# Raw x transposed before the row factor, small loads on ScalarE's queue, and a new order for a planned kernel

## The chip, the cores and the metric

The kernel runs on 1 core of one Trainium2 chip. The metric is the time of one execution in microseconds on the device, lower is better. The time before is 354.06 us, the median of 3 runs.

## The reference

A trunk of two layers on x (256 tokens, width 1024): an RWKV-7 time mixing with 16 heads of 64, and a block-sparse attention that, with 256 tokens and blocks of 256, is plain causal attention within one block. All in float32. What matters here, cut:

```python
def rms_norm(x, g):
    y = xf * lax.rsqrt(jnp.mean(xf * xf, axis=-1, keepdims=True) + RMS_EPS)
    return y * g
...
def rwkv7_time_mix(h, mu, w_in, ...):            # h = rms_norm(x, norm_a)
    xx = jnp.pad(h, ((0, 0), (1, 0), (0, 0)))[:, :-1] - h        # the token before, minus this one
    # six inputs (h + xx * mu[i]) @ w_in[...]: r, w (64 wide), k, v, a (64 wide), gate
    w = -softplus(-(w0 + tanh(wdn) @ w2)) - 0.5;  decay = exp(-exp(w))
    a = sigmoid(a0 + adn @ a2)
    ...                                           # kk normed per head, k scaled by a
    def step(S, inp):                             # a scan over the 256 tokens, state 64 x 64 per head
        S = S * d_t - (S kk_t) b_t + v_t k_t;  y = S r_t
    ...                                           # group norm, bonus, silu gate
    return y @ w_out
...
x = x + rwkv7_time_mix(rms_norm(x, norm_a), ...)
kb, vb, kmean = shared_kv(x, ...)                 # rms_norm(x) @ w_kv
x = x + moba_attention(rms_norm(x, norm_b), ...)  # (softmax(q k) v * silu(gate)) @ w_out
```

## The kernel before

The work is written as some hundreds of small generators ("parts"). Each yields operations, events and buffer requests; a planner, the class Weave, runs them against a model of the engines while the kernel is built, and emits each operation when its model starts it. So the order of the instructions on every engine, and which of two engines takes an operation that may go to either, come from the planner's costs, from the priority with which a part is spawned (lower first) and from a table of numbers (PR) and a few constants (ORDER_A, FIRST, ALT, STICK, WARM and others) at the end of the file. On the chip the order is fixed: every engine runs its list from the front, and waits where an operand is not ready. One line (L308) issues nearly all VectorE, ScalarE and GpSimd instructions, L413 the products, L417 the transposes on TensorE, L424 the loads; so rows are told apart by the names of their tiles.

The tokens are two blocks of 128 (b = 0, 1), the columns two halves of 512 (n or q = 0, 1), called halves of the heads.

*The head.* block(b) squares x's two halves on ScalarE (sq, with the sum in ssq), adds the two sums on VectorE (rs) and takes the power -1/2 on GpSimd. In the kernel before, normed(b, q, r) multiplies x by that factor (xn), transposes xn on TensorE in four pieces, and multiplies by norm_a while it copies the result to hT (tokens along the free axis; VectorE for q = 0, ScalarE for q = 1). xxT is hT of the token before minus hT. start() turns the rows of norm_a and mu_a into columns (vrow to vT), and forms wm, the two 64-wide weights wl times mu. The low-rank products (low_rank) take hT with wl and xxT with wm, 16 per block, and the "rate" products w2x with their result give decay (sw) and a (ia).

*The mixed inputs.* For the key k, z = hT + xxT * mu is formed per block and 256 rows (u, SCALAR_TENSOR_TENSOR) and split into a high part (zhi, ScalarE, rounded to fp32r) and a low part (zlo, VectorE). The weights come in quarters of 256 x 512 (raw), split in the same way (whi, wlo). A dense job sums three products per tile: whi zlo, wlo zhi, whi zhi. The input v is not split but multiplied in plain fp32 ("raw" with zhi and zlo as places).

*The rest.* Each half of the heads goes through transposes of alpha (the tile called sw by then), the forms M1 and M2 (kkh and ia) and rho (eL), products within chunks of 64 tokens (WL, BK), the inverse of the triangular matrices (XF, tmp, xw on VectorE; ZX, QS on TensorE, with products of 16, 32 and 64 rows), and the recurrence over four chunks. Then come the output projection, the sums (x), K, V, Q and gate, the scores, softmax, values, and the last projection. warm_up() fills TensorE with products of zeros at the beginning. Loads go out on SyncE's queue in the planner's order, and a load into a buffer waits there until the buffer is free.

*Names:* whi/wlo, zhi/zlo: high and low parts; con: the constants (identity in its first 128 columns); acc and ps: PSUM buffers; rs: row factor; bv: a vector spread over all partitions.

## Time and profile before

| | before |
|---|---|
| median of 3 runs | 354.06 us (353.94 to 358.91) |
| profiled execution | 354.56 us |
| its span, first to last instruction | 352.7 us |
| TensorE busy (PE) | 342.2 us, 97% |
| VectorE busy (DVE) | 286.6 us, 81% |
| ScalarE busy (ACT) | 211.1 us, 60% |
| GpSimd busy (POOL) | 46.7 us, 13% |
| chain that ended last, by engine | PE 82%, DVE 13%, DMA 1%, issue 1% |

Busy times count an instruction from its start to its modelled end, and neighbours overlap; where a row gives 0.39 us for a product, the next one may start 0.23 us later. A row of a timeline gives the start, the length and, in brackets, the idle time of the engine before it and what ended it. [...] A plain fp32 product of the program appears as two records.

### The profile page before, as it was taken

Reading aid. Unit: us, or ns where it says so; the run is one execution under the profiler, and the core shown is the slowest. Engines: PE = TensorE matmul, PEld = TensorE weight load, DVE = VectorE, ACT = ScalarE, POOL = GpSimd, SP = SyncE. Lnnn points to the kernel's source line nnn. Section 1 sums busy time; section 2 is a strip of 40 time slices with the busy share of each in tenths; the row PEclk is TensorE's granted clock in tenths of the full one; section 3 lists DMA queues with packets and bytes.
Section 4 is the critical chain, followed back from the end, with each engine's and each line's share of the span. In section 5 each row is a group of like instructions: output and inputs, shape, how many; then the busy total and the mean of one; then the engine's idle time right before and its main releaser. Section 6 shows DMA issues by size and latency. Waiting matters only on the chain.

```text
span 352.7 us, 7611 instructions
## 1 busy us (share of the span) xinstructions
PE 342.2 (97%) x3006; PEld 266.1 (75%) x3006; DVE 286.6 (81%) x572; ACT 211.1 (60%) x415; POOL 46.7 (13%) x71
## 2 busy tenths in 40 slices
PE   8798999999999999999999999999999999999995
PEld 8774877778466775568777788788888878889784
DVE  2899789999999869959769989648868987769823
ACT  5379986754247852265673556645578775688620
POOL 1200050000310000200220522005504005000000
PEclk9899999999999999999999999999999999999999
DMA  7674762673254912356535512565540266503603
GB/s 197 179 205 137 240 192 77 171 215 94 89 151 125 239 59 61 91 134 233 189 111 180 187 60 73 198 222 185 175 164 2 77 228 223 190 1 122 205 35 119
DMA packets 29740, 51.44 MB, mean 146 GB/s; under 512 B 4412, under 2 KB 5764, under 8 KB 29704
## 3 DMA queue, kind: packets, MB, share of 16 engines
q1 hardware_dynamic: 29704, 50.94, 47.4%
q8 instruction: 24, 0.39, 0.5%
q14 instruction: 12, 0.10, 0.1%
HBM read 48.31 MB, written 1.05 MB: 140 GB/s over the span
## 4 chain that ended last, share of the span: by engine, by line
PE 82%; DVE 13%; DMA 1%; issue 1%; POOL 0%; ACT 0%; SPq 0%; DVEq 0%
PE acc L413 56%; PE ps L413 19%; PE ps L417 6%; DVE u L308 3%; DVE wlo L308 2%; DVE zlo L308 1%; DMA tri<-in_consts_dram 1%; DVE z L308 1%; DVE k L308 1%; DVE x L308 1%; DVE xxT L308 1%; DVE tmp L308 1%; DVE kkh L308 1%; DVE XF L308 0%; POOL rs L308 0%
## 5 line engine op out<-in xcount | busy, mean ns | idle before, releaser
L308 DVE TENSOR_TENSOR wlo<-raw,whi 128x1024 fp32r<-128x1024 f32 x70 | 85.4, 1222 | 25.2 <-ACT whi L308 25.0
L308 ACT ACTIVATE whi<-raw 128x1024 fp32r<-128x1024 f32 x70 | 74.1, 1064 | 39.4 <-PE acc L413 23.7
L413 PE MATMUL acc<-wlo,zhi 128*128 128x512 f32 x120 | 51.6, 430 | 1.0 <-DVE wlo L308 1.0
L413 PE MATMUL acc<-whi,zlo 128*128 128x512 f32 x120 | 47.1, 393 | 0.6 <-DVE zlo L308 0.6
L413 PE MATMUL acc<-whi,zhi 128*128 128x512 f32 x120 | 47.1, 392 | 0.0
L413 PE MATMUL acc<-whi,z 128*128 128x512 f32 x128 | 39.8, 392 | 0.0
L413 PEld LDWEIGHTS acc<-wlo,zhi 128*128 128x128 f32 x120 | 22.5, 188 | 7.3 <-DVE wlo L308 1.4
L413 PEld LDWEIGHTS acc<-whi,z 128*128 128x128 f32 x128 | 24.1, 188 | 4.9
L413 PEld LDWEIGHTS acc<-whi,zhi 128*128 128x128 f32 x120 | 22.5, 188 | 5.0
L413 PEld LDWEIGHTS acc<-whi,zlo 128*128 128x128 f32 x120 | 22.6, 189 | 4.8 <-DVE zlo L308 0.9
L413 PE MATMUL acc<-wlo,z 128*128 128x512 f32 x64 | 26.0, 406 | 0.0
L413 PE MATMUL acc<-zb,whi 128*128 128x256 f32 x128 | 23.3, 282 | 0.0
L413 PE MATMUL acc<-whi,zb 128*128 128x512 f32 x64 | 20.0, 394 | 0.0
L413 PE MATMUL acc<-whi,zf 128*128 128x512 f32 x64 | 19.8, 390 | 0.0
L413 PEld LDWEIGHTS acc<-zb,whi 128*128 128x128 f32 x128 | 19.7, 189 | 0.1
L413 PE MATMUL acc<-zb,wlo 128*128 128x256 f32 x64 | 18.9, 295 | 0.0
L308 POOL TENSOR_TENSOR nrm<-nrm,half 128x8 f32<-128x8 f32 x4 | 8.1, 2021 | 78.0 <-DVE nrm L308 78.0
L413 PE MATMUL acc<-raw,zlo 128*128 128x512 f32 x32 | 15.5, 605 | 0.0
L413 PE MATMUL acc<-raw,zhi 128*128 128x512 f32 x32 | 15.0, 606 | 0.0
L413 PEld LDWEIGHTS acc<-wlo,z 128*128 128x128 f32 x64 | 12.1, 189 | 2.9 <-issue 0.5
L413 PEld LDWEIGHTS acc<-whi,zb 128*128 128x128 f32 x64 | 12.1, 189 | 2.6
L308 ACT ACTIVATE zhi<-u 128x256 fp32r<-128x256 f32 (+1 forms) x16 | 7.9, 522 | 10.1 <-DVE u L308 7.0
(215 smaller groups left out, 721.6 us busy)
## 6 DMA issues: line engine op xcount, KB each, us to landing
raw<-in_w_in_a_dram SPq DMA_DIRECT2D x32, 512.0 KB, 4.3
raw<-in_w_kv_dram SPq DMA_DIRECT2D x16, 512.0 KB, 3.7
raw<-in_w_in_b_dram SPq DMA_DIRECT2D x16, 512.0 KB, 4.2
raw<-in_w_out_a_dram SPq DMA_DIRECT2D x8, 512.0 KB, 4.9
raw<-in_w_out_b_dram SPq DMA_DIRECT2D x8, 512.0 KB, 4.5
x<-in_x_dram SPq DMA_DIRECT2D x8, 256.0 KB, 4.4
out_dram<-x SPq DMA_DIRECT2D x8, 128.0 KB, 1.9
NBK<-kkh SPq DMA_DIRECT2D x6, 128.0 KB, 5.8
```

What stands on the lines that cost most here:

```text
L308: op = Op(eng, us, lambda: getattr(obj, name)(*a, **k), table=table, banks=banks(*a, *k.values()), port=port(eng, name, us, a, k))
L413: return us, lambda: nc.tensor.matmul(dst, l, r, **kw), size(r) * (1 if l.dtype == F32R else 4) * min(l.shape[0], size(l)) / P, banks(dst) ...
L417: return max(0.045, 0.1085 * src.shape[0] / P), lambda: nc.tensor.transpose(dst, src, idt), 256 * src.shape[0] / P, banks(dst), src.shape[ ...
```

## The change

The row factor is put on after the transpose. turned(b, q) transposes raw x as soon as it is there and multiplies by norm_a on the way to hT; block(b) turns the row factor itself into a row, spread over all partitions (pr, one transpose), and normed(b, q, rT) multiplies hT by it in place, on VectorE. The loads of norm_a, mu_a and the identity are issued on ScalarE's queue, ahead of its table load. More parts take their priority from the table; the table, the job order of the first layer's v and g, that of the second layer, and the planner's constants have other values; warm_up() takes an acc buffer instead of a ps buffer. The step from 16 to 32 rows of the inverse is not changed, only the planner's cost of some of its products (0.031 to 0.033).

```diff
+    for a, b in ((vrow[0:8], norm_a[0].rearrange("(a p) -> a p", p=P)),
+                 (vrow[8:56], mu_a[0].rearrange("i (a p) -> (i a) p", p=P)), (con[:, 0:128], consts[0:P, 0:128])):
+        nc.scalar.dma_start(a, b)
+    warm = keep((P, 1), "warm")
+    nc.scalar.activation(warm, half[:, 0:1], AF.Tanh)
...
-            spawn(fetch(f"x{n}{b}", (xb[n, b], x2[b * P:(b + 1) * P, hs(n)])), -3)
+            spawn(fetch(f"x{n}{b}", (xb[n, b], x2[b * P:(b + 1) * P, hs(n)])), PR["x"] if b else -3)
...
-            spawn(load(i, raw, op), (-2.5, PR["raw1"], PR["raw2"])[i] if i < 3 else 0)
+            spawn(load(i, raw, op), PR[f"raw{i}"] if i < 5 else 0)
...
-    def normed(b, q, r):
+    def turned(b, q):
+
+        b1 = slice(b * P + 1, (b + 1) * P + 1)
+        yield event("ident")
+        yield event(f"x{q}{b}")
+        pt = yield bank
+        yield tr4(pt, xb[q, b])
+        yield event("vT")
+        yield either(V.tensor_tensor(hT[q][:, :, b1], pt.rearrange("p (a t) -> p a t", t=P), bc(na_T[:, q * 4:q * 4 + 4], P), op=ALU.mult),
+                     several([S.activation(hT[q][:, i, b1], pt[:, i * P:(i + 1) * P], AF.Copy, scale=na_T[:, q * 4 + i:q * 4 + i + 1])
+                              for i in range(4)]))
+        bank.give(pt)
+        fire(f"turned{b}{q}")
+
+    def normed(b, q, rT):
...
-        xn = T_(f"k2{q}{b}", "xn")
-        yield either(V.tensor_scalar(xn, xb[q, b], r, None, op0=ALU.mult), S.activation(xn, xb[q, b], AF.Copy, scale=r))
...
+        yield event(f"turned{b}{q}")
+        yield V.tensor_tensor(hT[q][:, :, b1], hT[q][:, :, b1], rT[:, 0:P].unsqueeze(1).to_broadcast([P, 4, P]), op=ALU.mult)
...
     def block(b):
+        for q in range(2):
+            spawn(turned(b, q), PR["block"] * b + 1)
         r = yield from norm_row(b)
-        yield event("vT")
-        for q in range(2):
-            spawn(normed(b, q, r), 1 + b)
+        pr = yield accs
+        yield pe(tr(pr[:, 0:P], r.to_broadcast([P, P]), ident))
+        ends = [spawn(normed(b, q, pr), PR["block"] * b + 1 + q * 0.1) for q in range(2)]
+        for e in ends:
+            yield e
+        accs.give(pr)
...
-PR = {"raw1": 2.8, "raw2": 95.8, "w2x": 25.7, "first": -19.5, "k0": -26.6, "r0": -29.4, "k1": 147.2, "r1": -16.2,
+PR = {"x": 26.1, "wl": -2.1, "raw0": 26.7, "raw1": 29, "raw2": 76.5, "raw3": -21.5, "raw4": 31.2, "lora": 56.8,
...
-ORDER_A = ("k0", "r0", "k1", "r1", "v0", "g0", "v1", "g1")
-FIRST = [(0, 1), (0, 0), (1, 1), (2, 1), (1, 0), (2, 0), (3, 0), (3, 1)]
+ORDER_A = ("k0", "r0", "k1", "r1", "v0", "v1", "g0", "g1")
+FIRST = [(0, 1), (0, 0), (1, 1), (1, 0), (2, 1), (2, 0), (3, 1), (3, 0)]
...
-COLD, WINDOW, KEEP, WARM = 1.9, 3.4133, 1046, (1.1, 9.16)
+COLD, WINDOW, KEEP, WARM = 1.9, 3.4133, 874, (1.1, 11.52)
...
-SWAP, STICK = 0.1, 0
+SWAP, STICK = 0.1, 56.9
```

VectorE's list at the very beginning, before (x_74 and x_76 are block 0, x_75 and x_77 block 1; hT_83 is the first half of the columns, xxT_85 its difference):

```order
L308 TENSOR_TENSOR rs_141<-ssq_98 128x1
L308 COPY vT_81<-ps_50_149 128x56
L308 TENSOR_SCALAR xn_153<-x_74,rs_141 128x512
L308 TENSOR_SCALAR xn_154<-x_76,rs_141 128x512
L308 TENSOR_TENSOR hT_83<-ps_54_160,vT_81 128x4x128
L308 TENSOR_TENSOR xxT_85<-hT_83 128x4x128
L308 TENSOR_TENSOR rs_177<-ssq_99 128x1
L308 SCALAR_TENSOR_TENSOR u_58_185<-xxT_85,vT_81,hT_83 128x128
L308 TENSOR_TENSOR xxT_86<-hT_84 128x4x128
L308 SCALAR_TENSOR_TENSOR u_58_185<-xxT_85,vT_81,hT_83 128x128
L308 SCALAR_TENSOR_TENSOR u_59_186<-xxT_85,vT_81,hT_83 128x128
L308 TENSOR_SCALAR xn_198<-x_75,rs_177 128x512
```

and now (x_72 and x_74 are block 0, x_73 and x_75 block 1; hT_86 and hT_87 the two halves, acc_53 the turned factor of block 0, rs_232 the factor of block 1):

```order
L308 COPY vT_84<-ps_49_138 128x56
L308 TENSOR_TENSOR rs_148<-ssq_101 128x1
L308 TENSOR_TENSOR hT_86<-ps_48_137,vT_84 128x4x128
L308 TENSOR_TENSOR hT_87<-ps_51_140,vT_84 128x4x128
L308 TENSOR_TENSOR hT_86<-hT_86,acc_53_158 128x4x128
L308 TENSOR_TENSOR hT_87<-hT_87,acc_53_158 128x4x128
L308 TENSOR_TENSOR xxT_88<-hT_86 128x4x128
L308 TENSOR_TENSOR wm_176<-wl_78,vT_84 128x8x64 x2
...
L308 TENSOR_TENSOR zlo_116<-u_62_202,zhi_115 128x2x128
L308 COPY vT_84<-ps_60_196 128x16
L308 TENSOR_TENSOR rs_232<-ssq_102 128x1
L308 TENSOR_TENSOR hT_86<-ps_67_234,vT_84 128x4x128
```

The steps on xn are gone, both halves of hT are formed on VectorE and multiplied there a second time, and the factor of block 1 stands behind the splits (zlo) of block 0, not in the middle of its work.

SyncE's list of loads, before (con_73 the identity, vrow_78 the rows of norm_a and mu_a, x_75 and x_77 block 1, raw_34, raw_35 and raw_36 the first three weight quarters):

```order
L424 DMA x_74<-in_x_dram 128x512
L424 DMA x_76<-in_x_dram 128x512
L424 DMA con_73<-in_consts_dram 128x128
L424 DMA vrow_78<-in_norm_a_dram 8x128
L424 DMA vrow_78<-in_mu_a_dram 48x128
L424 DMA x_75<-in_x_dram 128x512
L424 DMA x_77<-in_x_dram 128x512
L424 DMA wl_80<-in_w_in_a_dram 128x8x64 x2
L424 DMA raw_34_105<-in_w_in_a_dram 128x2x512
L424 DMA bv_33_104<-in_ka_a_dram 128x512
L424 DMA vrow_79<-in_norm_kv_dram 8x128
```

and now (x_73 and x_75 block 1, raw_34 and raw_35 the first two quarters; the third, raw_36, stands at place 25, behind raw_74 and raw_78, the fourth and fifth):

```order
L424 DMA x_72<-in_x_dram 128x512
L424 DMA x_74<-in_x_dram 128x512
L424 DMA wl_78<-in_w_in_a_dram 128x8x64 x2
L424 DMA bv_33_107<-in_ka_a_dram 128x512
L424 DMA vrow_77<-in_norm_kv_dram 8x128
L424 DMA vrow_77<-in_norm_b_dram 8x128
L424 DMA x_73<-in_x_dram 128x512
L424 DMA x_75<-in_x_dram 128x512
L424 DMA bv_59_188<-in_kk_a_dram 128x512
L424 DMA raw_34_108<-in_w_in_a_dram 128x2x512
```

Three small loads have left the list; wl, a bv and the two later gains stand ahead of block 1 of x, and another bv between it and the first weight quarter.

VectorE's list where alpha of the second half of the heads is formed, before (sw_335 is alpha of block 0; kkh_349 and kkh_458 the two blocks; tmp, XF, xw the inverse of the first half):

```order
L308 TENSOR_TENSOR kkh_349<-kkh_349,nrm_1050 128x512
L308 TENSOR_TENSOR tmp_981<-xw_983 128x512
L308 TENSOR_SCALAR nrm_1076<-nrm_1076 128x8
L308 TENSOR_TENSOR ia_336<-kkh_349,ia_336 128x512
L308 TENSOR_REDUCE XF_982<-tmp_981 128x64
L308 TENSOR_TENSOR sw_335<-kkh_349,sw_335 128x512
L308 TENSOR_TENSOR tmp_981<-xw_983,XF_982 128x512
L308 TENSOR_TENSOR kkh_349<-ia_336,enL_480 128x4x64
L308 TENSOR_REDUCE xw_983<-tmp_981 128x8x8
```

and now (sw_365 is alpha of block 0, kkh_355 and kkh_425 the two blocks):

```order
L308 TENSOR_TENSOR kkh_355<-kkh_355,nrm_1040 128x512
L308 TENSOR_REDUCE XF_984<-tmp_983 128x64
L308 TENSOR_TENSOR kkh_425<-kkh_425,nrm_1066 128x512
L308 TENSOR_TENSOR tmp_983<-xw_985,XF_984 128x512
L308 TENSOR_TENSOR ia_366<-kkh_355,ia_366 128x512
L308 TENSOR_REDUCE xw_985<-tmp_983 128x8x8
L308 TENSOR_TENSOR sw_365<-kkh_355,sw_365 128x512
L308 TENSOR_SCALAR XF_984<-xw_985,con_71 128x16x16 x2
L308 TENSOR_TENSOR ia_368<-kkh_425,ia_368 128x512
L308 STREAM_TRANSPOSE ZX_1115<-XF_984 128x16x2x16
L308 TENSOR_TENSOR sw_367<-kkh_425,sw_367 128x512
```

The norm factor of the second block, the second tmp and its reduction stand ahead of alpha of the first block now, and alpha of the second block follows close behind it.

## Rows read from the trace of the kernel before

**Rows 1.** The page, busy time of each engine, share of the span, instructions.

```profile
PE 342.2 (97%) x3006; PEld 266.1 (75%) x3006; DVE 286.6 (81%) x572; ACT 211.1 (60%) x415; POOL 46.7 (13%) x71
```

**Rows 2.** Stretches: length; busy of PE, PEld, DVE, ACT, POOL; PEclk; DMA share, GB/s.

```profile
8.90:12.30 3.40, 1.29 (x13) 1.13 (x12) 3.40 (x10) 1.77 (x4) 2.00 (x4) 1.00 0.93 290
12.30:15.70 3.40, 3.40 (x19) 3.40 (x18) 3.40 (x7) 0.43 (x2) 0.00 (x0) 0.50 0.42 158
15.70:19.10 3.40, 3.40 (x32) 3.40 (x32) 1.93 (x6) 1.43 (x5) 0.00 (x0) 1.00 0.56 148
...
60.00:80.00 20.00, 20.00 (x139) 15.80 (x138) 19.42 (x36) 13.88 (x34) 0.00 (x0) 1.00 0.62 171
```

**Rows 3.** Waits of TensorE: what for, us in total, times, longest us.

```profile
PE acc L413 <- DVE wlo L308: 1.0, 1, 1.0
PE ps L413 <- issue: 0.9, 1, 0.9
PE ps L417 <- DVE sw L308: 0.8, 1, 0.8
PE acc L413 <- DVE zlo L308: 0.6, 1, 0.6
PE ps L417 <- POOL rs L308: 0.3, 1, 0.3
```

**Rows 4.** Timeline of TensorE in the head: start, length, instruction, idle before it.

```profile
18.24 1.06 PE L413 MATMUL ps<-hT,wl 128*128 128x128 f32 x8
...
22.29 0.50 PE L413 MATMUL acc<-whi,zlo 128*128 128x512 f32 x1 [0.62 <-DVE zlo L308]
...
27.34 4.88 PE L413 MATMUL ps<-w2x,tl 65*128 65x512 f32 x11
...
32.96 0.40 PE L413 MATMUL acc<-whi,zhi 128*128 128x512 f32 x1
34.35 0.50 PE L413 MATMUL acc<-wlo,zhi 128*128 128x512 f32 x1 [0.99 <-DVE wlo L308]
```

**Rows 5.** Timeline of VectorE in the head.

```profile
5.01 0.16 DVE L308 TENSOR_TENSOR rs<-ssq 128x1 f32<-128x1 f32 x1 [4.03 <-ACT sq L308]
...
7.62 0.69 DVE L308 TENSOR_TENSOR hT<-ps,vT 128x512 f32<-128x512 f32 x1 [0.52 <-PE ps L417]
...
14.80 1.21 DVE L308 TENSOR_TENSOR wlo<-raw,whi 128x1024 fp32r<-128x1024 f32 x1
...
18.43 1.13 DVE L308 SCALAR_TENSOR_TENSOR u<-xxT,vT,hT 128x128 f32<-128x128 f32 x4
...
21.48 0.76 DVE L308 TENSOR_TENSOR zlo<-u,zhi 128x256 fp32r<-128x256 f32 x2
```

**Rows 6.** Timeline of ScalarE and of GpSimd in the head.

```profile
3.39 0.63 ACT L308 ACTIVATE sq<-x 128x512 f32<-128x512 f32 x1 [1.18 <-DMA x<-in_x_dram]
...
5.53 0.58 POOL L308 TENSOR_TENSOR rs<-rs,half 128x1 f32<-128x1 f32 x1
...
9.56 0.89 POOL L308 TENSOR_TENSOR rs<-rs,half 128x1 f32<-128x1 f32 x1
```

**Rows 7.** Timeline of SyncE's queue: start and length of each issue.

```profile
2.51 0.32 SPq L424 DMA_DIRECT2D vrow<-in_mu_a_dram  x1
...
26.06 0.39 SPq L424 DMA_DIRECT2D raw<-in_w_in_a_dram  x1
```

**Rows 8.** Timeline of TensorE around a group of narrow products.

```profile
48.60 0.39 PE L413 MATMUL acc<-whi,zhi 128*128 128x512 f32 x1
48.92 0.43 PE L417 MATMUL ps<-con,eL 32*128 32x32 f32 x8
49.28 0.50 PE L413 MATMUL acc<-wlo,zhi 128*128 128x512 f32 x1
49.62 0.39 PE L413 MATMUL acc<-whi,zlo 128*128 128x512 f32 x1
49.85 0.40 PE L413 MATMUL acc<-whi,zhi 128*128 128x512 f32 x1
```

**Rows 9.** Timeline of VectorE in the inverse of the first half.

```profile
97.52 1.10 DVE L308 TENSOR_TENSOR tmp<-xw,XF 128x512 f32<-128x512 f32 x1
```

More of the change, by code (lines that the diff above doesn't have):

```diff
@@ L487, in yoco @@
     nc.gpsimd.memset(half, -0.5)
-    warm = keep((P, 1), "warm")
-    nc.scalar.activation(warm, half[:, 0:1], AF.Tanh)
     con = keep((P, C_TRI), "con")
@@ L493, in yoco, with there @@
     wl = T_("ab", "wl", (P, KT, 2, 64))
+    for a, b in ((vrow[0:8], norm_a[0].rearrange("(a p) -> a p", p=P)),
[3 more added lines that the diff above has]
+    nc.scalar.activation(warm, half[:, 0:1], AF.Tanh)
+    def there(key, t):
+        yield t
+        fire(key)
+    spawn(there("ident", 4.3), -3)
+    spawn(there("vrow", 4.1), -3)
     def fetch(key, *pairs):
@@ L500, in fetch_first @@
         for n in range(2):
-            spawn(fetch(f"x{n}{b}", (xb[n, b], x2[b * P:(b + 1) * P, hs(n)])), -3)
+            spawn(fetch(f"x{n}{b}", (xb[n, b], x2[b * P:(b + 1) * P, hs(n)])), PR["x"] if b else -3)
     fetch_first(0)
-    spawn(fetch("ident", (con[:, 0:128], consts[0:P, 0:128])), -3)
-    spawn(fetch("vrow", (vrow[0:8], norm_a[0].rearrange("(a p) -> a p", p=P)),
-                (vrow[8:56], mu_a[0].rearrange("i (a p) -> (i a) p", p=P))), -3)
     fetch_first(1)
     spawn(fetch("wl", *((wl[:, :, i, :], w_in_a[0, :, c:c + 64].rearrange("(a p) f -> p a f", p=P))
-                        for i, c in enumerate((1024, 3136)))), -3)
+                        for i, c in enumerate((1024, 3136)))), PR["wl"])
     spawn(fetch("vrow2", (vrow2[0:8], norm_kv.rearrange("(a p) -> a p", p=P)),
@@ L745, in start @@
         wm = T_("z0", "wm", (P, KT, 2, 64))
-        spawn(lora(wm), 3)
+        spawn(lora(wm), PR["lora"])
         yield [vg("tensor_tensor", wm[:, :, which, :], wl[:, :, which, :], bc(vT[:, 8 + mi * 8:16 + mi * 8], 64), op=ALU.mult)
@@ L831, in lora @@
         for b in range(NB):
-            spawn(low_rank(b, wm, pls[b]), 3)
+            spawn(low_rank(b, wm, pls[b]), PR["lora"])
         for b in range(NB):
@@ L859, in lora @@
             for which in range(2):
-                spawn(rate(n, b, which), 3 + n * 0.5)
+                spawn(rate(n, b, which), PR["rate"] + n * 0.5)
     def decay(n):
@@ L1120, in inverse @@
         p3 = pq.rearrange("p (m t) -> p m t", t=32)
-        yield [pe(*(mm(p3[q * 64:q * 64 + 64, m, :], A[top, m, :], XN[top, m, :], 0.031, start=True, stop=True,
+        yield [pe(*(mm(p3[q * 64:q * 64 + 64, m, :], A[top, m, :], XN[top, m, :], 0.033, start=True, stop=True,
                       tile_position=(q * 64, q * 64)) for q, m, top, bot in tops[i:i + 8]))
@@ L1134, in inverse @@
         p3 = pz.rearrange("p (m t) -> p m t", t=32)
-        yield [pe(*(mm(p3[top, m, :], QS[bot, m, :], ZD[bot, m, :], 0.031, start=True, stop=True,
+        yield [pe(*(mm(p3[top, m, :], QS[bot, m, :], ZD[bot, m, :], 0.033, start=True, stop=True,
                       tile_position=(q * 64 + 32, q * 64)) for q, m, top, bot in tops[i:i + 8]))
@@ L1630, in warm_up @@
         yield WARM[0]
-        t = yield bank
+        t = yield accs
         while weave.now < WARM[1]:
             yield pe(mm(t[:, 0:P], z, z, 0.2155, start=True, stop=True))
-        bank.give(t)
+        accs.give(t)
     def zeros():
@@ L1641, in yoco @@
     for b in range(NB):
-        spawn(block(b), 1 + b)
-    spawn(start(), 0)
+        spawn(block(b), PR["block"] * b + 1)
+    spawn(start(), PR["wm"])
     spawn(late_gains(), 20)
@@ L1697 @@
 LAND = 2.3
-LEAST, SPARE = 4, -8.48
+LEAST, SPARE = 4, -8.72
 FOLLOW = -1e6
```

18 lines of the change are left out of this document (4 added, 14 removed), and 11 rows, old and new, of the table PR.

## The prediction

> **What bounds the kernel now.** I read the page's first part, then the stretches of the run, then what TensorE waited for, then the rows of the head engine by engine. TensorE is busy for 342.2 of 352.7 us and VectorE for 286.6 [rows 1]; in the stretch from 60 to 80 us TensorE is busy for all 20.00 us and VectorE for 19.42 [rows 2]. A wide product is issued every 0.23 us (49.62 to 49.85, [rows 8]), and nothing between 34.35 us and the tail opens a gap longer than about a microsecond. The list of TensorE's waits names the gaps: 1.0 us for a wlo, 0.9 us of "issue", 0.8 us for sw (alpha of the second half of the heads) and 0.3 us for rs [rows 3]. So the end is set by TensorE's work, which the change leaves as it is, plus three things: the time at which TensorE's dense stretch begins, the gaps in it, and what switching between kinds of product costs. The long products run without a stop from 22.29 us on, and the last wait of the head ends at 34.35 us, 0.99 us of idle in front of it [rows 4]. The tail is the same in both orders: the last twelve products of the output job, then four sums and their stores.
>
> **The head, part by part.** The first products of job k0 take block 1 of the tokens (FIRST begins with (0, 1) in both orders), so what matters is when block 1 is normed, mixed and split; block 0 matters only by what it puts ahead of block 1 on VectorE.
>
> *The small loads.* Three issues leave SyncE's queue and stand on ScalarE's, ahead of its table load: mu_a took 0.32 us [rows 7], and with the same or a little more for norm_a and the identity they are about 1.1 us. That is hidden: ScalarE idles 1.18 us in front of its first square, waiting for x [rows 6]. If x came earlier than the 3.39 us of that row, up to 0.5 us would show. [...]
>
> *Block 0.* The normed copy xn goes (it came after rs and ahead of the transposes), and instead the raw x is transposed and multiplied by the row factor afterwards. rs is added at 5.01 us [rows 5]; then hT twice, the factor twice, xxT twice and wm twice, 8 instructions of the kind that takes 0.69 us (0.60 from start to start) [rows 5], and the factor cannot start before the power ends at 6.11 [rows 6] and TensorE has turned it, about 6.5 us; 8 STT (1.13 us for four, about 0.27 each) and 4 zlo (0.76 for two, about 0.34 each) [rows 5] follow. That is 7.1 (factor on the second half), 7.7, 8.3, 8.9, 9.5 (xxT of the second half), 10.1, 12.2, 13.6 us.
>
> *Block 1.* Its x is now issued after wl, ka and two gains. About 1.6 MB land ahead of its end, from 3.39 us on; at the 290 GB/s of the stretch from 8.90 us it would end at 8.9, at the 158 of the next one, whose DMA engines were half idle (0.42), at 13.5 [rows 2]; I take 10, nearer the busy row. ScalarE reads the second half only behind the four zhi of block 0, so its square ends near 13.5 us, which hides the later x; were x later than 12.7 us, every microsecond would go straight to TensorE's start. VectorE adds rs near 13.7 us, and the way to the end of the power took 1.1 us for block 0 (5.01 to 6.11 [rows 5, 6]) and 0.3 more for block 1, whose power alone took 0.89 instead of 0.58 [rows 6], so that TensorE turns rs near 15.0 and VectorE goes on at 15.3. From there VectorE's order is two more factor or hT steps (to 16.5), wlo of 1.14 us [rows 5], xxT, factor, wlo, four STT: xxT of the second half starts at 21.05 and ends at 21.7 us. TensorE still has to put the last four low-rank products of block 1 behind that (8 records in 1.06 us at the full clock, 18.24 us, [rows 4]). So the dense stretch starts at 22.7 us at the earliest; with these products at the lower clock until some of the way, at 23.3. I take 22.9: **+0.6 us** against 22.29. Bounds: -0.3 (the power in 0.6 us and both blocks' steps without a wait) and +1.8 (all of them at the lower clock, 24.1).
>
> *The last wait of the head.* The third weight quarter (raw, kq 2) was issued at 26.06 us [rows 7]. In the new order it stands behind the fourth and fifth quarter too, but these wait for wlo of the first two, now 17.7 and 20.0 us; so it goes out near 22 us, four earlier, its whi stands near 31 us on ScalarE behind three sigmoids, and its wlo ends near 32.5 us on VectorE. TensorE has 15 products of 0.23 us, eight rate products of two records of 0.43 us each (11 records in 4.88 us) [rows 4] and nine more products ahead of it, 12.3 us, and comes at 35.2. So the 0.99 us of [rows 4], with the slower start behind it (34.35 - 32.96 - 0.23), **-1.2 us**; at worst nothing of it goes. What is late next there is VectorE, about 2.5 us ahead of TensorE, which is the cover.
>
> **The rest of the run.** The numbers and priorities only set an order: all counts of instructions are as before but for the 4 xn, 8 ScalarE steps on hT, 2 hT and 4 factor steps, two turned rs and 18 instead of 20 products with zero, all of it in the head (the zeros fill a TensorE that waits anyway; if it did not, two fewer would save 0.4 us). What the new order changes is the switches. A group of narrow products costs 0.09 us on the way in (48.60 to 48.92 is 0.32 where 0.23 is usual) and 0.11 us on the way out (49.28 to 49.62) [rows 8]. I count 46 such groups before and 44 now, and 31 returns from transposes to wide products before and 27 now, at 0.09 each: 2 x 0.20 + 4 x 0.09, **-0.7 us** rounded down for the head's own. Lower bound -0.8, upper 0.
>
> *The gaps at 97 and 107 us* [rows 3]. TensorE turns alpha of the second half in order. In the new order VectorE does three more steps ahead of that alpha (the norm factor of the other block, a tmp of 1.10 us [rows 9] and its reduction, 2.2 us with 0.60 for each of the other two), but TensorE too comes to it about 2 us later, having more v products in front. Between these I take no change: **0**. If VectorE is the later one by all of it, +2.2; if the new order covers both gaps, -1.7. The gap for rs (0.3 us [rows 3]) I leave.
>
> **The sum.** +0.6 - 1.2 - 0.7 + 0 = -1.3 us. The profiled execution took 354.56 us in all (352.7 of span and 1.9 around it), so 353.3; the median of the three runs, 354.06, is 0.5 lower, which gives **352.8 us** for the changed kernel.
>
> **The rivals.**
> 1. *The clock falls in the hole that block 1 now leaves (slower).* Between 8.90 and 12.30 us TensorE was busy for 1.29 of 3.40 us, and the granted clock of the next 3.4 us was 0.50, 1.2 GHz; it was 1.00 again after a stretch that was busy throughout [rows 2]. In the new order TensorE has next to nothing to do between 12.1 and 15.0 us, and then low-rank products with waits between them. If the lower clock lasts into the dense stretch, it starts at 24.1 us and runs at half rate for some 3.4 us, which costs 1.7: +1.8 + 1.7 - 1.2 - 0.7 is +1.6; 354.56 + 1.6 - 0.5 is **355.7 us**. It decides once TensorE starts its dense stretch at 1.2 GHz. For it: the hole is longer than the one before. Against: the low-rank products fill most of the 3.4 us ahead of 22.5. [...] Chance 0.22.
> 2. *VectorE becomes the bound at alpha of the second half.* The 2.2 us above show in full: 353.3 + 2.2, less 0.5, **355.0 us**. For it: VectorE is at 19.42 of 20 us [rows 2]. Chance 0.13.
> 3. *All gaps close.* Start as before, no wait in the head, none at 97, 107 and 221 us: -1.2 - 1.7 - 0.3 - 0.7 is -3.9, 350.7 against the profiled run's own time and **350.2 us** against the median. Chance 0.12.
> 4. *The change does not do what it says:* the raw transposes end earlier, the row factor ends no earlier, and the third quarter waits as long as before: **354.1 us**. Chance 0.05.
>
> **Chances and range.** My forecast has 0.48, with a range of its own from 351.3 to 354.3. With rivals 1 and 2, and most of 3, the range that should hold the time 8 times in 10 is 350.0 to 356.0 us. Two per cent of 354.06 is 7.1 us, about what a measurement of this kernel can tell from no change; no case above reaches 347.0 or 361.1. I give 0.02 to faster, since the gaps after 22.29 us are 1.2 + 0.8 + 0.9 + 0.3, 3.2 us in all, 0.94 to the same and 0.04 to slower, where the first two rivals meet with a late transfer.
>
> **What would show it.** Right: TensorE's first unhindered long product at 22.6 to 23.3 us; no wait for wlo near 34 us; the squares of block 1's x well apart, the second behind four zhi; the waits for sw and "issue" near 100 us together within 1 us of the 1.7 they had. Wrong: a granted clock of 0.5 after 22.5 us (rival 1); a wait for sw or ZX of over 2 us near 100 us (rival 2); a square of block 1 that waits for its x later than 12.7 us; or a wait for weights after 40 us, which no step above expects.

## The result: slower by 0.7 per cent

The changed kernel takes 357.23 us (median of 20 runs, 354.94 to 361.96), the kernel before, run beside it, 354.46 us (20 runs). The ratio is 1.0074, with a 95% interval from 1.0051 to 1.0096: slower, by less than two per cent. Ratios and their intervals compare the runs that lie within 1.5% of the fastest run of the same kernel; medians are over all runs. The prediction was 352.8 us with a range from 350.0 to 356.0, so the time lies outside it, on the side of the first rival.

The profiled execution took 358.33 us, with a span of 356.5 us, 3.8 more than before. The page's first part and the line of TensorE's granted clock in its second part (PEclk: tenths of the full clock, 9 for 90% or more), of the changed kernel:

```profile
PE 344.1 (97%) x3004; PEld 267.6 (75%) x3004; DVE 288.8 (81%) x574; ACT 207.9 (58%) x407; POOL 47.9 (13%) x71
...
PEclk9989999999999999998999999999999999999999
```

TensorE is busy 1.9 us longer than in [rows 1], for as much work: its clock was down in two stretches, where the kernel before had one [rows 2]. TensorE's waits, which answer to [rows 3]:

```profile
PE ps L413 <- DVE hT L308: 1.8, 1, 1.8
PE ps L417 <- DMA con<-in_consts_dram: 1.5, 1, 1.5
PE ps L413 <- issue: 1.1, 1, 1.1
PE acc L413 <- DVE zero L308: 1.0, 1, 1.0
PE ps L417 <- DVE sw L308: 1.0, 1, 1.0
PE ps L417 <- DVE rs L308: 1.0, 1, 1.0
```

The wait for wlo is gone, as forecast. New are the identity (con), hT and rs, all in the head (in a second execution the wait for rs is put down to vT; VectorE does the two one behind the other, at 15.86 and 15.95 us). TensorE's timeline in the head, against [rows 4]:

```profile
5.90 0.32 PE L417 MATMUL ps<-con,vrow 56*128 56x56 f32 x1 [1.51 <-DMA con<-in_consts_dram]
6.16 1.97 PE L417 MATMUL ps<-con,x 128*128 128x128 f32 x8
...
21.29 1.16 PE L413 MATMUL ps<-hT,wl 128*128 128x128 f32 x8 [1.82 <-DVE hT L308]
...
24.08 2.07 PE L413 MATMUL ps<-xxT,wm 128*128 128x128 f32 x8 [0.23 <-DVE xxT L308]
25.80 0.61 PE L413 MATMUL acc<-wlo,zhi 128*128 128x512 f32 x1
```

The long products begin at 25.80 us. The last low-rank products (eight records) took 2.07 us, where eight records took 1.06 at the full clock [rows 4]. VectorE's rows say where the lateness was made, against [rows 5]:

```profile
6.26 0.22 DVE L308 COPY vT<-ps 128x56 f32<-128x56 f32 x1 [5.28 <-PE ps L417]
...
8.80 1.28 DVE L308 TENSOR_TENSOR hT<-hT,acc 128x512 f32<-128x512 f32 x2
...
14.52 1.41 DVE L308 TENSOR_TENSOR zlo<-u,zhi 128x256 fp32r<-128x256 f32 x4
...
15.95 0.14 DVE L308 TENSOR_TENSOR rs<-ssq 128x1 f32<-128x1 f32 x1
...
23.34 0.68 DVE L308 TENSOR_TENSOR xxT<-hT 128x512 f32<-128x512 f32 x1
```

From 8.80 us until behind the start of the long products VectorE has no idle time over 0.7 us: the whole chain is late because it began late. The stretches around the two falls of the clock (length, busy of PE, PEld, DVE, ACT, POOL, then the granted clock, DMA share, GB/s):

```profile
19.25:22.67 3.42, 1.60 (x14) 1.41 (x14) 3.42 (x6) 0.00 (x0) 0.00 (x0) 1.00 0.41 104
22.67:26.08 3.41, 3.18 (x16) 2.89 (x15) 3.41 (x12) 1.45 (x5) 0.00 (x0) 0.50 0.95 299
159.20:162.60 3.40, 2.28 (x135) 1.72 (x133) 2.37 (x4) 3.29 (x9) 0.00 (x0) 1.00 0.68 236
162.60:166.10 3.50, 3.50 (x39) 2.64 (x39) 2.82 (x6) 1.69 (x5) 0.00 (x0) 0.51 0.02 7
```

Each fall, to a granted clock of 0.50 and 0.51, follows a stretch in which TensorE was not busy for 1.82 of 3.42 us and for 1.12 of 3.40. The trace gives the clock as a share; what the prediction calls 1.2 GHz is a share of 0.50. The second fall is in the inverse of the second half; TensorE's rows there:

```profile
160.05 0.61 PE L413 MATMUL ps<-ZX,QS 32*32 32x16 f32 x50
161.78 0.84 PE L413 MATMUL ps<-ZX,QS 32*32 32x16 f32 x78 [1.12 <-issue]
162.55 1.10 PE L413 MATMUL ps<-UV,WL 128*64 128x64 f32 x16
163.59 0.80 PE L413 MATMUL acc<-wlo,zhi 128*128 128x512 f32 x1
164.18 0.63 PE L413 MATMUL acc<-whi,zlo 128*128 128x512 f32 x1
164.61 0.63 PE L413 MATMUL acc<-whi,zhi 128*128 128x512 f32 x1
```

In the middle of one group of 128 narrow products TensorE waits 1.12 us for nothing that the profile shows ("issue"; by the experiments on the count, below, its place goes with the count of TensorE's records), and the products behind it run slower: 16 in 1.10 us (0.69 at the full clock, below), and two of 512 columns start 0.43 us apart (164.18 and 164.61), where 0.23 is usual. That no step of the prediction had.

**Where the 3.8 us are.** An estimate from the products' rows of both traces: each product's start, less the unhindered time of all products since the first long one. What is left over is lost in waits, switches and clock. The bounds are microseconds of such work since the first long product. Before, the first long product came at 21.17 us and waited again until 22.29, where the prediction's sum begins. "Three causes" and "before, held" are two kernels of the experiments below.

| us | before | after | difference | three causes | before, held |
|---|---|---|---|---|---|
| first long product starts | 21.17 | 25.80 | +4.63 | 23.81 | 19.40 |
| lost from 0 to 20 | 2.43 | 0.39 | -2.04 | 0.25 | 2.32 |
| lost from 20 to 110 | 5.27 | 4.71 | -0.56 | 4.48 | 5.24 |
| lost from 110 to 135 | 3.03 | 5.50 | +2.47 | 3.54 | 3.70 |
| lost from 135 to the end | 4.15 | 3.82 | -0.33 | 3.66 | 4.17 |
| unhindered work | 312.42 | 312.02 | -0.40 | 312.02 | 312.42 |

The head (first two lines) cost +2.6 us, and the place near 160 us, which lies in 110 to 135 us of work, +2.5.

### The profile page after: what moved, and what is told of

The parts are those of the page before. It is cut to its first block, busy times and chain, and to the rows that moved or that the text cites. A ratio compares the mean times of both kernels' runs of the same rounds, so it can differ in the third digit from the quotient of the medians.

```text
span 356.5 us, 7607 instructions
## 1 busy us (share of the span) xinstructions
PE 344.1 (97%) x3004; PEld 267.6 (75%) x3004; DVE 288.8 (81%) x574; ACT 207.9 (58%) x407; POOL 47.9 (13%) x71
## 4 chain that ended last, share of the span: by engine, by line
PE 85%; DVE 10%; issue 1%; DMA 1%; ACT 0%; ACTq 0%; DVEq 0%
PE acc L413 60%; PE ps L413 18%; PE ps L417 7%; DVE u L308 2%; DMA con<-in_consts_dram 1%; DVE zlo L308 1%; DVE tmp L308 1%; DVE hT L308 1%; DVE wlo L308 1%; DVE kkh L308 1%; DVE xw L308 1%; DVE RR L308 1%; DVE xxT L308 1%; DVE WL L308 1%; DVE XF L308 0%
## 5 line engine op out<-in xcount | busy, mean ns | idle before, releaser
L413 PEld LDWEIGHTS acc<-whi,z 128*128 128x128 f32 x128 | 24.1, 188 | 4.9
L308 ACT ACTIVATE zhi<-u 128x256 fp32r<-128x256 f32 (+1 forms) x16 | 7.9, 520 | 16.6 <-DVE u L308 16.5
L308 ACT ACTIVATE AB<-ps 32x256 f32<-32x256 f32 (+1 forms) x32 | 10.3, 322 | 7.8 <-PE ps L413 6.3
L308 ACT ACTIVATE UV<-ps 64x256 f32<-64x256 f32 x8 | 3.0, 379 | 19.8 <-PE ps L413 16.4
```

The lines of the kernel that those rows point to most:

```text
L308: op = Op(eng, us, lambda: getattr(obj, name)(*a, **k), table=table, banks=banks(*a, *k.values()), port=port(eng, name, us, a, k))
L413: return us, lambda: nc.tensor.matmul(dst, l, r, **kw), size(r) * (1 if l.dtype == F32R else 4) * min(l.shape[0], size(l)) / P, banks(dst) ...
```

## The experiments

The theories: the identity comes late on ScalarE's queue; the clock falls; VectorE is the bound whatever TensorE does. A fourth, the count of instructions, came with the traces. Ratios are to the kernel before on the same chip. The edits are shown shortened, some of them in words.

**Small loads back on SyncE.**

```diff
-        nc.scalar.dma_start(a, b)          # norm_a, mu_a, identity
+        nc.sync.dma_start(a, b)            # the same, behind block 0's x
```

> The changed kernel with one part undone: identity, norm_a and mu_a are issued on SyncE behind block 0's x, as before the change; every engine's order of other work is that of the changed kernel (357.2 us). Late identity: it lands near 4.4 us instead of 5.8, the whole chain on VectorE in the head moves ahead by 1.3 us, the first long product comes near 24.5 instead of 25.8 us, and the time is about 355.9 us or, where the half-clock stretch at 22.7 us then falls elsewhere, up to 1 us less. Clock alone: the hole between the low-rank products stays, the half clock stays at 22.7 to 26.1 us, the first long product stays within 0.5 us of 25.8, and the time is 356.7 to 357.2 us. VectorE as the bound: the same start does not matter, 357.2 us.

Measured: 355.71 us, ratio 1.0021 [0.9989, 1.0053]. TensorE's rows:

```profile
5.19 0.24 PE L417 MATMUL ps<-con,vrow 56*128 56x56 f32 x1 [0.93 <-DMA vrow<-in_mu_a_dram]
5.35 1.09 PE L417 MATMUL ps<-con,x 128*128 128x128 f32 x8
...
24.25 0.57 PE L413 MATMUL acc<-wlo,zhi 128*128 128x512 f32 x1
```

The transposes start 0.71 us earlier and the long products 1.55. Not all of that is the loads': the eight transposes ran at the full clock here (1.09 us, not 1.97), and so they did in a second execution of the changed kernel, with the identity as late as ever (below). The half clock still came here too, at 21.05 us. Ahead of it TensorE had the last xxT at 22.52 us, that second execution at 23.34 and the first trace at 24.08:

```profile
22.52 2.07 PE L413 MATMUL ps<-xxT,wm 128*128 128x128 f32 x8 [0.18 <-DVE xxT L308]
```

So the loads delay the chain by 0.8 us at equal clock, and the first transposes at half clock by another 0.7.

**Identity first on ScalarE's queue.**

```diff
-    for a, b in (norm_a, mu_a, identity):
+    for a, b in (identity, norm_a, mu_a):
```

> The changed kernel with the identity first of the three loads on ScalarE's queue instead of last; nothing else moves. Late identity (because it is issued behind two loads and behind wl): it lands at 3.5 to 4.7 us, the first transposes at 4.8 instead of 5.9 us, the first long product 1.1 us earlier, the time near 356 us. If the queue, not the place in it, makes it late: it lands after 5.3 us and the time stays at 357.2 us. Clock alone: first long product within 0.5 us of 25.8.

Measured: 356.64 us, ratio 1.0015 [0.9983, 1.0046], and

```profile
5.81 0.32 PE L417 MATMUL ps<-con,vrow 56*128 56x56 f32 x1 [1.42 <-DMA vrow<-in_mu_a_dram]
```

The identity was there at 4.0 us, but mu_a now at 5.7: whichever of the three is last is late. The order on ScalarE's queue only changes which of them TensorE waits for; on SyncE's queue, ahead of wl, the last had landed at 5.05 us (run above). Here wl is issued on SyncE at 1.62 us, beside them, and lands at 6.1 and 7.2; whether that is what holds them up no run separates. The ratios do not tell this kernel from the one above; the medians, on one chip, differ by 0.93 us.

**Clock held in the head.** The extra products go to the bank in which block 1's low-rank sums are being built, each with a start of its own; this kernel leaves out part of those sums and serves for its times alone.

```diff
+        if (key, b, q) == ("hT", 1, 0):
+            for c in (384, 384, 256):
+                nc.tensor.matmul(pl[:, P:P + c], ident, xb[1, 1][:, 0:c], start=True, stop=True)
```

> The changed kernel with three extra plain products (384, 384 and 256 columns, some 1.7 us, into columns that nobody reads) behind the first four low-rank products of block 1, where TensorE idled from 19.5 to 21.3 us. Clock: the granted clock is 1.00 from 22.5 us on, the first long product comes near 24.9 instead of 25.8 us, the time falls by 0.9 to 1.1 us to 356.2 us. Late identity: the chain on VectorE sets the start whatever the clock, first long product within 0.3 us of 25.8, 357.2 us. Against both, the extra products delay the low-rank ones: 0.3 us later than 25.8, 357.5 us.

Measured: 356.64 us, ratio 1.0026 [0.9991, 1.0061]; full clock from 9.37 us on in the head, first long product at 25.23 us although the identity's wait ended 0.23 us later than in the changed kernel's trace: 0.8 us for the half clock at 22.67. The first transposes again took 1.97 us.

**Clock held near 160 us.**

```diff
+    for op in the four groups of ZX,QS (32 x 16) of the second half:
+        two products of tri_r with itself (256 columns) ahead of each
```

> The changed kernel with eight extra products of 256 columns among the 64 narrow ones (32 x 16) of the inverse of the second half near 160 us, two ahead of each group of 16; they cost some 0.9 us of TensorE, less whatever of the 1.1 us wait for issue there they cover. Clock: no half clock at 162.6 to 166.1 us, 1.7 us less for 0 to 0.9 more, so 355.5 to 356.4 us, and the runs lie closer together. If the half clock there has another cause (a phase that moves with the start of the program): it stays in some runs and the time is 357.2 to 358.1 us.

Measured: 356.80 us, ratio 1.0037 [1.0003, 1.007]. No wait for issue is left, and the clock stays at 1.00:

```profile
162.15 0.44 PE L413 MATMUL ps<-ZX,QS 32*32 32x16 f32 x32
162.52 0.69 PE L413 MATMUL ps<-UV,WL 128*64 128x64 f32 x16
```

Of 5.5 us lost from 110 to 135, 2.7 are left, but by the same estimate the eight products cost 1.5 us with their switches. So both the wait and the half clock behind it can be taken away, but not for nothing in this way: the time missed the 355.5 to 356.4 us of the first case, and the runs did not lie closer together (355.87 to 363.56).

**One part alone, raw x transposed:** the changed kernel's turned(), normed() and block() with the loads, priorities, orders and constants of before.

```diff
-PR = {"x": 26.1, "wl": -2.1, ...}          # the table of the change
+PR = {"x": -3, "wl": -3, "block": 1, ...}  # the table of before
```

> One part of the change alone: raw x transposed and the row factor put on later; loads, priorities, orders and constants as in the kernel before (first long product there at 22.3 us, its median against itself 1.000). If the new order makes the late start: block 1 is turned and multiplied as early as before, the first long product comes at 21.5 to 22.8 us and the ratio is 0.998 to 1.002. If the part itself does it (four more steps of 0.6 us on VectorE and the second hT moved there from ScalarE): first long product at 24 us or later, ratio 1.004 to 1.007.

Measured: 378.22 us, ratio 1.0646 [1.059, 1.0702]. Both expectations missed. Its waits:

```profile
PE ps L413 <- issue: 5.1, 3, 3.6
PE ps L417 <- DVE rs L308: 3.3, 1, 3.3
PE acc L417 <- POOL rs L308: 3.1, 1, 3.1
PE ps L417 <- DVE sw L308: 2.8, 1, 2.8
```

The clock was at one half for 24 us in four stretches. A table of numbers belongs to the graph that it was made for; under another graph the planner gives another order throughout, so this run doesn't price the part.

**The other part alone, the order:** the row factor ahead of the transposes and the loads on SyncE, with the changed kernel's table.

```diff
-            spawn(turned(b, q), PR["block"] * b + 1)
+            spawn(normed(b, q, r), PR["block"] * b + 1)   # xn first, as before
```

> The other part alone: priorities, orders and constants of the change with the row factor ahead of the transposes and the small loads on SyncE as before. If the new order makes the late start: rs of block 1 comes behind the splits of block 0, the first long product at 24 us or later, ratio 1.004 to 1.007. If raw x transposed makes it: first long product at 22 to 23 us, ratio 0.996 to 1.000 (the wait for wlo at 34 us gone).

Measured: 360.82 us, ratio 1.0102 [1.0026, 1.0178]; xn of block 1 is waited for 1.97 us, and the first long product comes at 24.87 us. Behind that wait the clock is down from 16.92 to 23.74 us:

```profile
19.22 3.62 PE L413 MATMUL ps<-hT,wl 128*128 128x128 f32 x16
```

These take 1.95 us at the full clock, and the xxT,wm products behind them 2.48 instead of 1.95, so up to 2.2 us of the late start are the clock's. Block 1's late place makes a hole and a late start without raw x transposed; but this too is the table under another graph, so it does not price the order either.

**Block 1 early, loads on SyncE.**

```diff
-PR = {"x": 26.1, ... "block": 9.5,
+PR = {"x": -3, ... "block": 1,
```

> The changed kernel with block 1's x loaded behind block 0's and its steps at the priority of before, and the small loads back on SyncE. If the place of block 1 behind the splits of block 0 makes the hole: the last xxT ends near 15 us instead of 24, no half clock between 20 and 26 us, first long product at 21.5 to 22.5 us, time 353.5 us, ratio 0.997 to 1.001. If VectorE is the bound whatever the order: the long products start earlier but wait for zlo and wlo up to 35 us, and the time is 355 to 356 us, ratio 1.002 to 1.005.

Measured: 375.31 us, ratio 1.0519 [1.0444, 1.0593]. The last xxT ends at 16.5 us and the first long product comes at 21.50, as expected; but the clock stays down for 20 us. Stretches of this kernel, columns as above:

```profile
19.99:23.40 3.41, 1.59 (x8) 0.94 (x7) 3.41 (x10) 1.85 (x7) 0.00 (x0) 1.00 0.91 241
23.40:26.82 3.42, 3.42 (x7) 1.67 (x6) 3.42 (x12) 1.55 (x4) 0.00 (x0) 0.50 0.93 246
...
33.64:37.06 3.42, 3.42 (x5) 1.35 (x4) 2.88 (x4) 2.21 (x4) 0.00 (x0) 0.50 0.28 72
...
40.47:43.88 3.41, 3.41 (x9) 2.64 (x9) 0.00 (x1) 2.62 (x5) 0.00 (x0) 0.50 0.13 49
43.88:47.30 3.42, 3.42 (x16) 2.80 (x16) 1.83 (x2) 2.70 (x5) 0.00 (x0) 1.00 0.10 13
```

TensorE is busy throughout from 23.40 us on and its granted clock stays at 0.50 until 43.88: from 28.67 to 38.1 us it runs plain fp32 rate products (twelve records in 10.44 us), and the clock came back behind a stretch of long fp32r products. Here the early start was worth nothing, with a hole right in front of such products. That the hole is the cause is not shown: this kernel also has waits of 2.7 us for sw and 2.5 for issue, so this run does not price block 1's place.

**The changed kernel again.**

```diff
(no edit)
```

> The changed kernel unchanged, on this chip, for comparison: ratio 1.005 to 1.010. The clock: of the runs with a mean clock of 0.998 or more the span is 353 to 354 us, of those at 0.993 to 0.995 it is 354.5 to 356, so that one stretch at half clock costs 1 to 2 us. If the clock does not matter: no difference between these groups.

Measured: 356.97 us, ratio 1.0072 [1.0041, 1.0103]. In this trace the clock did not fall in the head:

```profile
6.18 1.09 PE L417 MATMUL ps<-con,x 128*128 128x128 f32 x8
...
23.34 1.16 PE L413 MATMUL ps<-xxT,wm 128*128 128x128 f32 x8 [0.74 <-DVE xxT L308]
24.26 0.48 PE L413 MATMUL acc<-wlo,zhi 128*128 128x512 f32 x1
```

```profile
18.71:22.12 3.41, 1.59 (x15) 1.57 (x15) 3.41 (x7) 0.00 (x0) 0.00 (x0) 1.00 0.42 116
22.12:25.54 3.42, 2.68 (x19) 2.27 (x18) 3.42 (x13) 1.64 (x6) 0.00 (x0) 1.00 0.95 281
```

The same program, the identity as late, 1.54 us earlier: 0.7 us because the first transposes ran at the full clock, 0.8 because the last low-rank products did. In the first trace 1.60 us of work was followed by half clock, here 1.59 was not; these rows do not tell the two apart. Later the clock did fall here too, from 165.48 to 168.89 us, behind a wait for issue of 0.69 us. Over all runs of both kernels, spans at a mean clock of 0.998 or more have their median at 351.6 us before (25 of 110 runs) and 353.6 after (4 of 32); at 0.992 to 0.997, at 353.0 and 355.4. On this chip alone, at 0.992 to 0.997, it is 353.1 and 355.3. So the change costs 2.0 to 2.4 us at equal clock, and besides it makes runs at full clock rarer.

**The kernel before, clock held in the head.**

```diff
+        eight more products of zeros at the end of warm_up()
```

> The kernel before with eight more products of zeros (some 1.9 us) at the end of its warm-up, in the hole of 2.1 us ahead of block 1's transposes; nothing else moves. Clock: no half clock at 12.3 to 15.7 us, the sixteen hT,wl products take 1.95 us instead of 3.07, the first unhindered long product comes at 21.0 to 21.6 instead of 22.3 us, and the time falls by 0.7 to 1.4 us, ratio 0.996 to 0.998. If VectorE sets the start of the dense stretch anyway: the clock is full but the long product comes at 22.2 us and the ratio is 0.999 to 1.001. If the extra products delay the transposes: ratio 1.001 to 1.003.

Measured: 354.24 us, ratio 0.9997 [0.9971, 1.0023]. The sixteen low-rank products took 1.95 us instead of 3.07, and the first unhindered long product came at 20.77 instead of 22.29 us [rows 4]. But the time stayed: the profile now has 1.18 us of waiting for RR at 121.30 us and 0.73 for issue at 160.46, where before had none. RR is VectorE's, yet VectorE is not what is late: it sat idle for 2.35 us, for AB of ScalarE, which had waited 2.68 us, until 117.66 us, for a weight quarter.

```profile
120.29 0.43 DVE L308 TENSOR_TENSOR WL<-ps,con 64x256 f32<-64x256 f32 x1 [2.35 <-ACT AB L308]
```

```profile
121.30 0.94 PE L413 MATMUL ps<-WL,BK 64*128 64x128 f32 x12 [1.18 <-DVE RR L308]
```

**The changed kernel, holes filled; then the same with the loads on SyncE.**

```diff
+        three (one) more zeros at 4.4 us, four at 14.7 us
+        two products of 512 columns at 19.5 us, into a free bank
```

> The changed kernel with its holes filled by products that nobody reads: three more zeros at 4.4 us, four at 14.7, two of 512 columns at 19.5; nothing else moves. Clock: full from 5 us on in the whole head, x's first transposes 1.1 us for eight, first long product at 24.1 to 24.4 us in the profiled run instead of 25.8, the runs closer together, time 356.0 us, ratio 1.003 to 1.005 (what is left is the longer chain on VectorE). If the clock is not what moves it: 357.0 us and ratio 1.006 to 1.008.

Measured: 357.91 us, ratio 1.0103 [1.005, 1.0157]. No half clock from 10.2 us on in the head, yet the first long product only at 25.38 us, because the transposes at 6.37 us still took 1.97, and near 160 us there are now two waits for issue, 0.76 and 0.57, with half clock from 167.22 us behind them. A miss for the clock alone.

> As the last, with the small loads back on SyncE behind block 0's x. Late identity and clock as two separate costs: first long product at 23.2 to 23.6 us, time 355.2 us, ratio 1.001 to 1.003. If the late identity only mattered through the clock: first long product at 24.1 us, ratio as in the run before this one.

Measured: 355.48 us, ratio 1.0022 [0.999, 1.0053]; full clock from 6.53 us to near the end, first long product at 23.96 us, between the two cases, with the ratio of the first; but again two waits for issue, at 159.40 (0.68) and 163.23 (0.75).

**Block 0 first.**

```diff
-FIRST = [(0, 1), (0, 0), (1, 1), (1, 0), (2, 1), (2, 0), (3, 1), (3, 0)]
+FIRST = [(0, 0), (1, 0), (2, 0), (0, 1), (1, 1), (2, 1), (3, 1), (3, 0)]
```

> The changed kernel with the first job's sums begun for block 0 instead of block 1: twelve long products (2.8 us) come ahead of block 1's last low-rank products, in the hole from 19.5 us on; VectorE's order in the head stays. If the start of the long products is what costs: first long product at 19.9 us, 1.5 to 2.5 us less than the changed kernel, 354.7 to 355.7 us, ratio 1.000 to 1.002. If VectorE is the bound: the time won is lost again by waits for zlo or wlo between 22 and 40 us, ratio 1.005 to 1.008. If the clock falls during the eight rate products, which now stand in a row: half clock somewhere from 24 to 34 us and 2 us or more slower than the changed kernel.

Measured: 380.44 us, ratio 1.0723 [1.0672, 1.0774]. The first long product comes at 20.15 us, and the third theory's case follows, larger than expected: a wait of 2.81 us for sw's buffer among the rate products, and half clock from 31.06 to 44.71 us and in three stretches later, beside a wait for issue of 3.74 us at 182.30.

**The count of instructions.** After 50 us the waits for issue of 0.5 us and more stand in all these traces at matmul records 719 (before, at 107.66 us), 1480 and 1607, give or take three, also where 6, 14, 16 or 18 records were put ahead or the order is another. They stay where the count is, not where the program is. (Two kernels have one of 0.7 us at their first rate products too, at 23.71 and 26.56 us.) 1480 and 1607 lie 127 records apart, 719 and 1480 six times that less one. Each record is a weight load and a product [rows 1], so 127 records are 254 instructions. What TensorE waits for there, no run here shows. Two kernels shift the narrow groups against the count:

```diff
+    16 tiny products (16 x 16) in TensorE's hole at 19.5 us     # +32 records
```

> The changed kernel with sixteen tiny products (16 x 16, two records each) that nobody reads in TensorE's hole at 19.5 us; nothing else moves. The wait belongs to the count of instructions: the waits for issue stay at records 720, 1480 and 1607, but these now fall 32 records earlier in the narrow groups; by the times between these records in the trace they grow from 1.2 us near 160 us to about 3 us, and the time is 1.5 to 2.5 us longer, 358.5 to 359.5 us, ratio 1.011 to 1.015. The wait belongs to the narrow products: it stays where it is in the program, ratio 1.006 to 1.009. The clock alone: no more than the ratio of before either.

Measured: 362.86 us (median of twelve runs), ratio 1.0108 [1.0045, 1.0172], which is not clear of the 1.0072 of the changed kernel itself. Nine of the twelve runs had a mean clock of 0.985 or less, against 3 of 32 of the changed kernel. TensorE near 160 us:

```profile
159.97 0.36 PE L413 MATMUL ps<-ZX,QS 32*32 32x16 f32 x18
161.68 1.11 PE L413 MATMUL ps<-ZX,QS 32*32 32x16 f32 x110 [1.35 <-issue]
...
165.25 0.58 PE L413 MATMUL acc<-whi,zlo 128*128 128x512 f32 x1 [1.42 <-issue]
...
168.09 3.62 PE L413 MATMUL ps<-ZX,AB 32*64 32x32 f32 x64
```

The wait comes 18 records into the group instead of 50, that is 32 earlier: exactly the shift, at record 1480 again. Together 2.77 us of waiting, and half clock from 164.28 to 174.52. So the trace shows the count; the ratio alone would not. The tiny products themselves ran in 0.96 us of a hole of 1.8.

```diff
-    nine products of zeros, 128 columns each
+    three of 384 columns                                        # -12 records
```

> The changed kernel with nine of its products of zeros (128 columns) made three of 384 columns: the same columns in twelve records less; nothing else moves. Count: the waits for issue near 160 us fall below 0.6 us together, so does the one at 110 us, the half clock behind them comes less often, time 355.6 to 356.4 us, ratio 1.003 to 1.006. Narrow products or clock: unchanged, 357.0 us.

Measured: 355.76 us, ratio 1.0032 [1.0012, 1.0052]. The wait is 0.19 us, 62 records into the group, and there is none at record 1607:

```profile
159.05 0.71 PE L413 MATMUL ps<-ZX,QS 32*32 32x16 f32 x62
159.95 0.74 PE L413 MATMUL ps<-ZX,QS 32*32 32x16 f32 x66 [0.19 <-issue]
```

Twelve records fewer, with not a column less of work, give back more than half of what the change had lost, if barely clear of the noise. Much of it is the clock: at a mean clock of 0.998 or more this kernel's spans have their median at 353.2 us (5 of 12 runs), the kernel before's on the same chip at 351.35. In the profiled execution the clock still fell, from 166.47 to 169.88 us.

**All three causes removed:** loads on SyncE, head filled, twelve records less.

> The changed kernel with the small loads on SyncE, its head filled with zeros and two products that nobody reads, and twelve records less than the changed kernel ahead of the narrow groups. If late identity, clock and count are the causes and add up: full clock, no wait for issue over 0.6 us near 160 us, time 354.0 to 354.8 us, ratio 0.998 to 1.001. If something else costs the rest: 355.5 us, ratio 1.002 or more.

Measured: 353.89 us, ratio 0.9988 [0.9963, 1.0013], all twelve runs at a mean clock of 0.997 or more. TensorE's group near 160 us runs through:

```profile
157.70 1.46 PE L413 MATMUL ps<-ZX,QS 32*32 32x16 f32 x128
```

**The kernel before with its clock held, at the old count.** Six products' worth of zeros more, not the eight of the run with the held clock:

```diff
-    eight more products of zeros
+    six products' worth of columns, in products of up to 384, no record more
```

> The kernel before with its clock held in the head (eight products' worth of zeros more, as in the run with the held clock) but no record more, since six zeros were put together into two of 384 columns and part of the new ones are as wide. If the count ate the gain of the held clock: no wait for issue at 160 us, span of the full-clock runs 351 to 352 us, time 353.0 to 353.8 us, ratio 0.995 to 0.998. If VectorE eats it: the wait for RR near 121 us stays at about 1.2 us, ratio 0.999 to 1.001.

Measured: 353.75 us, ratio 0.9986 [0.996, 1.0011]. The first unhindered long product is at 20.58 us, and the waits for RR and at 160 us are gone. Both repaired kernels have medians some 0.9 us under before's 354.74 on that chip (353.89 and 353.75); the intervals still hold 1. Between the two there is nothing: with its three causes removed the change is not slower than a kernel before that is helped in the same way, and not faster. By the table the repaired head still costs 2.3 us against that kernel (first product 4.4 us later, 2.1 less lost behind it), of which the rest of the run gives back 1.8; its last low-rank products still wait 0.7 us for xxT, so what is left there is the longer chain on VectorE.

## Why the prediction was wrong

- **The small loads**, costed at nothing. Wrong: the cover named was ScalarE's own idle time, while what counted was when the last of the three lands. TensorE's first transpose waited 1.51 us for the identity; by the run with the loads on SyncE that is 0.8 us of the chain at equal clock. The sum has no term for the loads; moving them cost time.
- **Block 0.** This is the step that failed first. The sum put hT right behind rs at 5.01 us and let the factor on the second half begin at 7.1; it began at 9.4. hT needs the transposes and vT, and VectorE's new list has the copy of vT ahead of rs; the kernel before had vT no earlier than this:

```profile
6.09 0.22 DVE L308 COPY vT<-ps 128x56 f32<-128x56 f32 x1 [0.93 <-PE ps L417]
```

  All that followed was 2.3 us late: xxT of the second half began at 11.81 us, not 9.5. With the loads on SyncE and the transposes at the full clock it began at 10.25, with the loads late and the full clock at 11.07. So 0.75 us is this step's own, 0.8 the loads', and 0.75 the half clock of the first transposes, which the profiled run had and the second execution had not.
- **Block 1.** x came by 9.5 us (10 predicted), so that was right. rs came at 15.95 (13.7 predicted), xxT of the second half ended at 24.0 (21.7): both late by what block 0 passed on. The order of steps was right; the start of the chain was not.
- **The start of the long products:** 25.80 us, not 22.9; 2.3 us is the chain's, the rest the clock's at 22.67 us.
- **The last wait of the head**, -1.2 us: right. It's gone, and what is lost in the first 20 us of work fell by 2.0, of which some 0.8 lies ahead of the 22.29 us where the sum began. The cover was thinner: the third quarter went out at 24.2 us, not near 22, and TensorE came later too.
- **Switches** -0.7: not borne out. From 20 to 110 us 0.56 less is lost, but the wait for issue of 0.85 us at 107.66 us left that stretch, so nothing of it need be the switches'. **The gaps at 97 and 107 us**, 0: the wait for sw is 1.0 us against 0.8 [rows 3], and the wait for issue moved away.
- **The 0.9 us of "issue"** [rows 3] was taken for a fixed gap. It is set by the count of instructions, and the change moved it from the first half's inverse into the second's, where the clock then fell: +2.5 us that no step had, 0.5 of it still there with the three causes removed.
- **Rival 1** happened in the profiled run, at its place, but only in part: the clock rose again at 26.08 us, so the 1.7 us for long products at half rate did not come. Its start of 24.1 us was 1.7 short, for the reason under Block 0. That the time came out near its 355.7 us is luck; the 2.5 us near 160 us were not in it. **Rival 2** did not happen: the wait for sw grew by 0.2 us only. Behind the head no run shows VectorE as the bound; the one wait that looked like it (for RR) came from a late weight quarter.

How much each cause carries is separated only in part. Spans at a mean clock of 0.992 to 0.997, against the kernel before on the same chip: the changed kernel +2.2 us, loads on SyncE +1.2, twelve records less +1.75. At 0.998 or more: loads on SyncE +0.7, twelve records less +1.85, all three causes removed +0.65. The changed kernels' medians are of 3 to 11 runs. So by these spans, at equal clock, the loads carry about half; the count costs mostly through the half clock behind its waits; and some 0.65 us stays open.

## What to carry to other kernels

Cost a moved load by when the last operand of the first dependent instruction lands, not by the idle time of the queue that issues it (here 0.8 us of the chain at equal clock). Where TensorE runs hundreds of tiny products in a row, count instructions: find the records at which it waits for issue, and shift the count with wider or fewer dummy products (here twelve records fewer took that wait from 1.12 to 0.19 us, 32 more from 1.12 to 1.35). Fill TensorE's holes where the full clock is wanted behind them, without adding records (11 of 12 runs of the kernel with all three causes removed had a mean clock of 0.998 or more, 25 of 110 of the kernel before). Compare traces, and repaired kernels, only at equal granted clock.

## What the hardware showed

- Busy time alone didn't bring the clock back in one kernel: TensorE was busy throughout from 23.40 to 43.88 us, with plain fp32 products of 65 rows for 12 us of it, and its granted clock was 0.50 all the while; it rose while long fp32r products ran, from 40.62 us on.
- Two runs of one program, TensorE busy for 1.59 and 1.60 us in the stretch ahead, were granted a clock of 1.00 and 0.50 in the next; with the first transposes at either clock as well, the long products started 1.54 us apart.
- A wait for issue sits at fixed counts of TensorE's records (719, 1480, 1607, give or take three) in all these kernels, over narrow products and wide ones alike; it cost nothing to 1.42 us in the changed kernel and its variants, and up to 3.74 us in kernels with another order. 32 tiny records in a hole moved it by exactly 32 places in the program.
